# Differential attention in a hybrid layer: the sample's heads in a stream of their own, q and k split once, both maps' scores in one tile

## The chip, the core and the metric

The kernel runs on one core of a Trainium2 chip. The metric is the device time of that core in microseconds, the median of several executions. One further execution is taken by the hardware profiler; the page and every view of the trace quoted here come from that one.

## What is computed

One step of a hybrid layer: 512 prompt tokens and 32 tokens of a sample with 512 cached positions, side by side in a width of 544 (`TOK`). A combined projection feeds branch A (differential attention), branch B (RWKV-7 time mixing) and gates; both branches are projected, merged, projected again, and a gated convolutional FFN follows. All of it is fp32. The change is in branch A, 8 heads, and in one helper that branch B uses too. What branch A computes for each head:

```python
def diff_attend(q, k, v, lam, mask):
    s = jnp.einsum('bqhcd,bkhcd->bchqk', q, k) * (DA_HEAD_DIM ** -0.5)
    if mask is not None:
        s = jnp.where(mask, s, -1e30)
    p = jax.nn.softmax(s, axis=-1)
    pd = p[:, 0] - lam * p[:, 1]
    return jnp.einsum('bhqk,bkhd->bqhd', pd, v)
...
    o = rmsnorm(o, da_subln) * (1.0 - lam_init)
    o_da = o.reshape(B, T, DA_WIDTH) @ w_o_da
```

`c` runs over the two softmax maps; q and k have 64 rows per map, v has 128. The prompt's queries go in four blocks of 128; block i sees keys 0 to 128(i+1), in chunks of 64 (`mask`). The sample's 32 queries see 512 cached and 32 new keys, with no mask.

## The kernel before, in words

**Products.** TensorE multiplies fp32 as three matmuls of a rounded part and a remainder (`hi`, `lo`). A dense product (`dense_g`, line 202) loads a weight tile of 128x512 on the SP queue (`wr`, three buffers), casts it on ScalarE (`wh`), subtracts on VectorE or GpSimd (`wl`) and issues the matmuls into `psd`. Its rows read `psd<-…`.

**The planner.** `Flow` (line 93) runs generators, called streams. A stream yields the time at which it may go on, or a mark it waits for; when no stream is due, `Flow` takes one step of dense work. The time is a model's (`PE.now`). In the attention the dense work is first what is left of the gates' and the input's projections (`fillers`), then `orw_g` (branch B's output projection, its input loaded by `load_z`). A scheduler behind it reorders instructions on each engine by its own model; the built order is then fixed.

**Attention** (`attention`, line 1308) is one stream. For each head h: `tokens` transposes v; for each block i, `scores` (line 1284) issues, for each map m, two matmuls into a PSUM tile of its own (`sc0`, `sc1`, each one bank), a mask write, a maximum (line 1298), an exponential with a sum (line 1299); then the pair is combined to `pd`. While that runs, `weighted` transposes the block before (`pdt`) and multiplies by v into `po`; after block 3 `attend_norm` (line 1113) takes the root of the mean square by an integer guess and four Newton steps (`rsqrt_tiny`, line 260). `finish_head` transposes the normed head (`on`) and puts it as `dh`, `dl` (`put_z`) for the last projection, `w_oda`. The pool `ap` has one buffer for each name where none is given.

**Loading a head** (`load_head`, line 1253). q and k lie in DRAM as 128 rows a head, 64 for each map. For each map m the rows are loaded twice, to both halves of a tile: Q holds the rounded part in one half and the remainder in the other, so that one matmul against K's rounded part in both halves takes two of the three products:

```python
for f in (hi, lo):
    nc.sync.dma_start(out=raw[f, :], in_=d[h, hi, :])
x = ap.tile([128, TOK], F32R, name=f"x{n}{m}")
A.copy(out=x, in_=raw)
if t == 0:
    V.tensor_tensor(out=x[lo, :], in0=raw[lo, :], in1=x[lo, :].bitcast(F32), op=ALU.subtract)
```

That is eight loads of 64x544 and v, four casts and four differences a head, with a raw tile and a cast tile for each of q and k and each map (`rQ0`, `xQ0`, `rK0`, `xK0`, …). For K the raw tile becomes the remainder (`rK` in `sc<-rK,xQ`). `load_head(h + 1)` is called after head h's scores, and the planner adds 6.5 us before the next scores may come.

**The sample** (`attend_sample(g)`, line 1177) handles four heads at once, packed in quarters of the partitions. It is called inside the same stream after heads 3 and 7, after `weighted` and `finish_head` of that head; `load_caches` loads the keys (`kc`). It uses the same PSUM tiles `sc0`, `sc1` and `po`.

**The start.** `load_z` (line 1126) loads eight tiles `zr` (two buffers), casts each and subtracts on GpSimd.

Of the kernel before, what the change touches and what calls it, by code (L numbers as in the profile page):

```python
# [26 lines left out]
SEQ = 512  # L27
# [134 lines left out]
def tile_hybrid_layer(  # L162
# [97 lines left out]
    def rsqrt_tiny(pool, x, n, tag):  # L260

        p = x.shape[0]
        yt = pool.tile([128, 16], F32, name=tag + "y", bufs=2)
        tt = pool.tile([128, 16], F32, name=tag + "t", bufs=2)
        y, t = yt[:p, :n], tt[:p, :n]
        V.tensor_scalar(out=y.bitcast(I32), in0=x.bitcast(I32), scalar1=-0.5, scalar2=1597463007.0,
                        op0=ALU.mult, op1=ALU.add)
        for _ in range(4):
            V.tensor_tensor(out=t, in0=y, in1=y, op=ALU.mult)  # L269
            V.scalar_tensor_tensor(out=t, in0=t, scalar=-0.5, in1=x, op0=ALU.mult, op1=ALU.mult)  # L270
            V.scalar_tensor_tensor(out=y, in0=t, scalar=1.5, in1=y, op0=ALU.add, op1=ALU.mult)
        return y
# [839 lines left out]

    def attend_norm(po, rz0, n):

        ssq = ap.tile([128, 4], F32, name="ssq", bufs=2)
        on = ap.tile([128, 4, 128], F32, name="on")
        for i in range(n):
            A.activation(out=on[:, i, :], in_=po[:, i, :], func=AF.Square, scale=rz0[:, i:i + 1], accum_out=ssq[:, i:i + 1])
        V.tensor_scalar(out=ssq[:, :n], in0=ssq[:, :n], scalar1=128.0 * EPS, scalar2=None, op0=ALU.add)
        rr = rsqrt_tiny(ap, ssq[:, :n], n, "at")  # L1120
        V.tensor_tensor(out=rr, in0=rr, in1=rz0[:, :n], op=ALU.mult)
        V.tensor_tensor(out=on[:, :n], in0=po, in1=rr.unsqueeze(2).to_broadcast([128, n, 128]), op=ALU.mult)
        return on


    def load_z(pool, src, h, l, eng):
        for k in range(KT):
            zr = pool.tile([128, TOK], F32, name="zr", bufs=2)
            nc.sync.dma_start(out=zr, in_=src[k])
            A.copy(out=h[:, k, :], in_=zr)  # L1130
            eng.tensor_tensor(out=l[:, k, :], in0=zr, in1=h[:, k, :].bitcast(F32), op=ALU.subtract)
# [45 lines left out]
    def attend_sample(g):  # L1177
# [6 lines left out]
        yield PE.now + 1.0  # L1184
        sc = [pssc.tile([128, 512], F32, name=f"sc{m}") for m in range(2)]
        kc = caches[g]
        for e, hh in enumerate(hs):
            for m in range(2):
                PE.matmul(sc[m][32 * e:32 * e + 32, :], qks[m * 64:m * 64 + 64, 0, hh, :],
                          kc[m * 64:m * 64 + 64, e, :], start=True, stop=True,  # L1190
# [9 lines left out]
        nm = ap.tile([128, 2], F32, name="nm", bufs=3)  # L1200
        nm2 = ap.tile([128, 2], F32, name="nm2")
        for m in range(2):
            V.tensor_reduce(out=nm[:, m:m + 1], in_=sc[m], axis=AX.X, op=ALU.max, negate=True)
            V.tensor_reduce(out=nm2[:, m:m + 1], in_=scn[m][:, 0:32], axis=AX.X, op=ALU.max, negate=True)
# [4 lines left out]
        for m in range(2):  # L1209
            A.activation(out=E[:, m, 0:PAST], in_=sc[m], func=AF.Exp, bias=nm[:, m:m + 1], scale=1.0,  # L1210
                         accum_out=Z4[:, 0, m:m + 1])
# [22 lines left out]
        A.copy(out=pdtn, in_=ps[0:32, 0:128])  # L1234
        yield max(PE.now + 1.5, po_free[0])
        po = pssc.tile([128, 4, 128], F32, name="po")
        Q4 = [slice(32 * e, 32 * e + 32) for e in range(4)]
# [4 lines left out]
        for e, q in enumerate(Q4):  # L1242
            PE.matmul(po[q, 0, :], pdtn[:, q], vs[:, e, :], start=False, stop=True, tile_position=(0, 32 * e))
        on = attend_norm(po[:, 0:1, :], rz1[:, 0:1], 1)
        po_free[0] = PE.now + 4.0
        yield PE.now + 5.0
# [6 lines left out]
    def load_head(h):  # L1253

        vt = ap.tile([128, TOK], F32, name="vt")
        nc.sync.dma_start(out=vt, in_=v_d[h])
        Q, KH, KL = [], [], []
        for m in range(2):
            hi, lo = slice(m * 64, m * 64 + 64), slice(64 - m * 64, 128 - m * 64)
            for t, (d, n) in enumerate(((q_d, "Q"), (k_d, "K"))):  # L1260
                kept = ap.tile([128, TOK], F32R if t else F32, name=f"r{n}{m}")
                raw = kept.bitcast(F32) if t else kept
                for f in (hi, lo):
                    nc.sync.dma_start(out=raw[f, :], in_=d[h, hi, :])
                x = ap.tile([128, TOK], F32R, name=f"x{n}{m}")
                A.copy(out=x, in_=raw)
                if t == 0:
                    V.tensor_tensor(out=x[lo, :], in0=raw[lo, :], in1=x[lo, :].bitcast(F32), op=ALU.subtract)
                    Q.append(x)
                else:  # L1270
                    V.tensor_tensor(out=kept, in0=raw, in1=x.bitcast(F32), op=ALU.subtract)
                    KH.append(x)
                    KL.append(kept)
        return vt, Q, KH, KL

# [8 lines left out]
    def scores(i, Q, KH, KL, rz):  # L1284

        nk = 128 * (i + 1)
        sc = [pssc.tile([128, 512], F32, name=f"sc{m}") for m in range(2)]
        nm = ap.tile([128, 2], F32, name="nm", bufs=3)
        E = ap.tile([128, 2, 512], F32, name="E", bufs=2)
        Z = ap.tile([128, 4], F32, name="Z", bufs=3)  # L1290
        for m in range(2):
            qb = slice(i * 128, (i + 1) * 128)

            n = max(nk, 256)
            PE.matmul(sc[m][:, 0:n], Q[m][:, qb], KH[m][:, 0:n], start=True, stop=False)
            PE.matmul(sc[m][:, 0:n], Q[m][:, qb], KL[m][:, 0:n], start=False, stop=True)
            V.memset(sc[m][0:64, nk - 64:nk], -1e30)
            V.tensor_reduce(out=nm[:, m:m + 1], in_=sc[m][:, 0:nk], axis=AX.X, op=ALU.max, negate=True)
            A.activation(out=E[:, m, 0:nk], in_=sc[m][:, 0:nk], func=AF.Exp, bias=nm[:, m:m + 1], scale=1.0,
                         accum_out=Z[:, m:m + 1])  # L1300
# [8 lines left out]
    def attention():  # L1309
# [36 lines left out]
        nxt = load_head(0)  # L1346
        load_caches(0)
        yield PE.now + 9.0
        for h in range(HEADS):
            vt, Q, KH, KL = nxt  # L1350
            vtok = tokens(vt)
            rz = ap.tile([128, 4, 2], F32, name="rz", bufs=2)
            for i in range(4):
# [8 lines left out]
                prev = h, i, pd, ready, vtok, rz  # L1362
            if h + 1 < HEADS:
                nxt = load_head(h + 1)
                sc_free = max(sc_free, PE.now + 6.5)
            if h % 4 == 3:
                yield from weighted(*prev)
                prev = None
                yield from finish_head()
                yield from attend_sample(h // 4)  # L1370
                if h + 1 < HEADS:
                    load_caches(h // 4 + 1)

    flow.run([attention()], att_dense)
    att_dense.finish()
# [286 lines left out]
```

## Time and profile before

| | us |
|---|---|
| median of the three runs | 1378.87 |
| the runs | 1372.31, 1378.87, 1379.1 |
| the profiled execution | 1372.92 |
| its span in the trace | 1371.1 |
| mean granted TensorE clock | 0.942 |
| TensorE busy in the span | 1271.1 (93%) |
| VectorE, ScalarE, GpSimd busy | 884.9, 587.3, 229.6 |

The page's 40 slices are 34.3 us each. The attention is in slices 19 to 26, some 627 to 868 us. A digit is the busy share of an engine in tenths; PEclk the granted clock in tenths. The chain that ended last is 75% TensorE and 14% VectorE:

```profile
PE   7799999799989999998898977799999999999996
PEclk9999888799989899999899996799999999999999
```

### The profile page before, as it was taken

The numbers are of one execution on the slowest core, as the hardware profiler recorded it, in microseconds if no ns is written. First come the engines' busy times: TensorE is split into PE (matmuls) and PEld (weight loads), VectorE is DVE, ScalarE is ACT, GpSimd is POOL, SyncE is SP. The second block draws the span as 40 slices with busy tenths as digits, with TensorE's granted clock in tenths as the row PEclk, the third lists the DMA queues.
The fourth block names the chain that finished last, engine by engine and source line by source line (L and its number), as shares of the span: only waits on it lengthen the run. The fifth ranks groups of instructions, "written<-read, shape, count | busy, mean of one in ns | idle before, by whom it ended". The sixth has DMA issues, their size and how long they took to land.

```text
span 1371.1 us, 29786 instructions
## 1 busy us (share of the span) xinstructions
PE 1271.1 (93%) x12014; PEld 1206.1 (88%) x12014; DVE 884.9 (65%) x1835; ACT 587.3 (43%) x1184; POOL 229.6 (17%) x264
## 2 busy tenths in 40 slices
PE   7799999799989999998898977799999999999996
PEld 7798898798878899988798964799999999999996
DVE  6857559765779233862767675566878778873323
ACT  5655544464412333334664464234544444453220
POOL 6600102111213101224202100000111111111111
PEclk9999888799989899999899996799999999999999
DMA  5255555154685354537662530345222222234321
GB/s 173 77 162 161 166 172 164 59 152 131 204 257 172 93 144 125 165 102 219 181 200 91 158 95 32 97 157 165 95 86 86 93 85 90 88 112 140 102 79 65
DMA packets 135465, 178.01 MB, mean 130 GB/s; under 512 B 41248, under 2 KB 64416, under 8 KB 135328
## 3 DMA queue, kind: packets, MB, share of 16 engines
q1 hardware_dynamic: 122256, 154.86, 37.5%
q10 hardware_dynamic: 13072, 21.26, 4.7%
q8 instruction: 94, 1.54, 0.5%
q14 instruction: 43, 0.35, 0.1%
HBM read 138.39 MB, written 37.41 MB: 128 GB/s over the span
## 4 chain that ended last, share of the span: by engine, by line
PE 75%; DVE 14%; ACT 4%; issue 3%; DMA 2%; POOL 1%; SPq 0%; DVEq 0%; ACTq 0%; POOLq 0%
PE psd L88 59%; PE misc L88 5%; PE psq L88 3%; PE psy L88 2%; PE po L88 2%; PE sc L88 2%; PE tp L92 1%; PE misc L92 1%; DVE XT L680 1%; DVE itmp L489 1%; DMA q_d<-qt 1%; DVE NP L635 1%; DVE Xp L491 1%; DMA zr<-z_d 1%; DVE att L269 0%
## 5 line engine op out<-in xcount | busy, mean ns | idle before, releaser
L218 ACT CAST wh<-wr 128x512 fp32r<-128x512 f32 (+1 forms) x316 | 193.1, 617 | 368.1 <-PE psd L88 321.4
L88 PE MATMUL psd<-h_h,wh 128*128 128x272 f32 x976 | 300.5, 308 | 0.4
L88 PE MATMUL psd<-h_h,wl 128*128 128x272 f32 x976 | 292.7, 301 | 2.8 <-POOL wl L219 2.6
L88 PE MATMUL psd<-h_l,wh 128*128 128x272 f32 x976 | 293.3, 301 | 0.2 <-DVE h_l L443 0.2
L219 DVE TENSOR_TENSOR wl<-wr,wh 128x512 fp32r<-128x512 f32 x230 | 157.4, 688 | 114.1 <-ACT wh L218 109.1
L88 PE MATMUL psd<-xgh,wl 128*128 128x272 f32 x704 | 204.0, 290 | 0.0
L88 PE MATMUL psd<-xgh,wh 128*128 128x272 f32 x704 | 203.0, 288 | 0.0
L88 PE MATMUL psd<-xgl,wh 128*128 128x272 f32 x704 | 202.2, 287 | 0.0
L88 PEld LDWEIGHTS psd<-h_h,wh 128*128 128x128 f32 x976 | 193.7, 198 | 6.2 <-issue 2.3
L88 PEld LDWEIGHTS psd<-h_h,wl 128*128 128x128 f32 x976 | 193.0, 198 | 5.3 <-POOL wl L219 3.0
L88 PEld LDWEIGHTS psd<-h_l,wh 128*128 128x128 f32 x976 | 193.9, 199 | 2.8 <-issue 1.4
L219 POOL TENSOR_TENSOR wl<-wr,wh 128x512 fp32r<-128x512 f32 x86 | 120.6, 1406 | 400.3 <-ACT wh L218 327.7
L88 PEld LDWEIGHTS psd<-xgl,wh 128*128 128x128 f32 x704 | 132.7, 188 | 0.0
L88 PEld LDWEIGHTS psd<-xgh,wl 128*128 128x128 f32 x704 | 132.3, 188 | 0.0
L88 PEld LDWEIGHTS psd<-xgh,wh 128*128 128x128 f32 x704 | 132.2, 188 | 0.1
L88 PE MATMUL psd<-ah,wh 128*128 128x272 f32 x352 | 101.7, 289 | 0.0
L88 PE MATMUL psd<-ah,wl 128*128 128x272 f32 x352 | 101.5, 288 | 0.0
L88 PE MATMUL psd<-al,wh 128*128 128x272 f32 x352 | 101.4, 288 | 0.0
L88 PE MATMUL psd<-mh,wh 128*128 128x272 f32 x256 | 76.2, 298 | 0.0
L88 PE MATMUL psd<-mh,wl 128*128 128x272 f32 x256 | 74.7, 292 | 0.0
L88 PE MATMUL psd<-ml,wh 128*128 128x272 f32 x256 | 74.6, 291 | 0.0
L1460 POOL COPY cvo<-uf 128x2 f32<-128x2 f32 x88 | 36.8, 449 | 220.3 <-DVE uf L1457 220.3
(366 smaller groups left out, 2592.8 us busy)
## 6 DMA issues: line engine op xcount, KB each, us to landing
wr<-w_in SPq DMA_DIRECT2D x132, 256.0 KB, 3.1
wr<-w_up SPq DMA_DIRECT2D x88, 256.0 KB, 2.8
wr<-w_down SPq DMA_DIRECT2D x40, 256.0 KB, 2.7
bkL<-bk_d SPq DMA_DIRECT2D x16, 512.0 KB, 5.0
ar_d<-ar SPq DMA_DIRECT2D x8, 544.0 KB, 3.1
t_d<-qt ACTq DMA_DIRECT2D x16, 272.0 KB, 2.9
rQ<-q_d SPq DMA_DIRECT2D x32, 136.0 KB, 3.8
rK<-k_d SPq DMA_DIRECT2D x32, 136.0 KB, 2.9
```

The source lines that it names most:

```text
L88: ins = self.pe.matmul(out, lhsT, rhs, **kw)
L92: ins = self.pe.transpose(out, in_, ident)
L218: A.copy(out=wh[:, :n], in_=raw)
L219: le.tensor_tensor(out=wl[:, :n], in0=raw, in1=wh[:, :n].bitcast(F32), op=ALU.subtract)
L489: V.tensor_tensor(out=tv, in0=X[:, :, 0:i, 0:i], in1=N[:, :, i, 0:i].unsqueeze(2).to_broadcast([128, 2, i, i]), op=ALU.mult)
L491: V.tensor_reduce(out=X[:, :, 0:i, i], in_=tv, axis=AX.X, op=ALU.add)
L635: V.transpose(out=xz[r0:r0 + 32].rearrange("p m a -> p a m"), in_=Xp[r0:r0 + 32, 0:16, :])
L680: V.transpose(out=XT[r0:r0 + 32, :, 32 * b:32 * b + 32].rearrange("p m i -> p i m"), in_=Xp[r0:r0 + 32].rearrange("p a i -> p i a"))
L1460: G.tensor_copy(out=cvo[:, t, :, w], in_=u[:, 512 + w::32])
```

## The change

1. `rsqrt_tiny` takes three Newton steps instead of four. It is used in `attend_norm`, in branch B's group norm and for its sample.
2. `load_z`: `zr` has one buffer instead of two.
3. `load_head`: q and k are each loaded once as 128x512 (`raw`), cast (`hi`) and subtracted (`lo`) once, and twelve copies of 64x512 between on-chip tiles, on the SP queue, place the parts (four for `Q`, eight for `KH` and `KL`). All six tiles have one buffer. It is called for h+1 at the start of head h, and the 6.5 us are gone.
4. `scores`: both maps lie in one PSUM tile of two banks; one mask write and one maximum serve both, and the exponentials come after.
5. `samples()` is a second stream: sample 0 is due after head 1's scores, sample 1 after head 4's; it loads its own caches. Its product goes to the pool of transposes (`tp`) instead of `po`, and its normed tile has a name of its own (`son`).

```diff
-        for _ in range(4):
+        for _ in range(3):
...
-            zr = pool.tile([128, TOK], F32, name="zr", bufs=2)
+            zr = pool.tile([128, TOK], F32, name="zr")
...
-        sc = [pssc.tile([128, 512], F32, name=f"sc{m}") for m in range(2)]
+        sc = pssc.tile([128, 2, 512], F32, name="sc")
...
+        V.tensor_reduce(out=nm, in_=sc, axis=AX.X, op=ALU.max, negate=True)
         for m in range(2):
-            V.tensor_reduce(out=nm[:, m:m + 1], in_=sc[m], axis=AX.X, op=ALU.max, negate=True)
...
-        yield max(PE.now + 1.5, po_free[0])
-        po = pssc.tile([128, 4, 128], F32, name="po")
+        yield PE.now + 1.5
+        po = misc().rearrange("p (a v) -> p a v", a=4)
...
-        Q, KH, KL = [], [], []
...
+        x = {n: ap.tile([128, 2, SEQ], F32R, name=n) for n in ("Q", "KH", "KL")}
+        F = [slice(0, 64), slice(64, 128)]
+        for d, places in ((q_d, (("Q", 0), ("Q", 1))), (k_d, (("KH", None), ("KL", None)))):
+            raw = ap.tile([128, SEQ], F32, name="raw")
+            nc.sync.dma_start(out=raw, in_=d[h, :, 0:SEQ])
+            hi, lo = [ap.tile([128, SEQ], F32R, name=n) for n in ("hi", "lo")]
+            A.copy(out=hi, in_=raw)
+            V.tensor_tensor(out=lo, in0=raw, in1=hi.bitcast(F32), op=ALU.subtract)
+            for m in range(2):
+                for part, (n, flip) in zip((hi, lo), places):
+                    for f in range(2) if flip is None else ((m + flip) % 2,):
+                        nc.sync.dma_start(out=x[n].bitcast(F32)[F[f], m, :], in_=part.bitcast(F32)[F[m], :])
+        return vt, x["Q"], x["KH"], x["KL"]
...
         for m in range(2):
-            qb = slice(i * 128, (i + 1) * 128)
-
-            n = max(nk, 256)
-            PE.matmul(sc[m][:, 0:n], Q[m][:, qb], KH[m][:, 0:n], start=True, stop=False)
-            PE.matmul(sc[m][:, 0:n], Q[m][:, qb], KL[m][:, 0:n], start=False, stop=True)
-            V.memset(sc[m][0:64, nk - 64:nk], -1e30)
-            V.tensor_reduce(out=nm[:, m:m + 1], in_=sc[m][:, 0:nk], axis=AX.X, op=ALU.max, negate=True)
-            A.activation(out=E[:, m, 0:nk], in_=sc[m][:, 0:nk], func=AF.Exp, bias=nm[:, m:m + 1], scale=1.0,
+            PE.matmul(sc[:, m, 0:n], Q[:, m, qb], KH[:, m, 0:n], start=True, stop=False)
+            PE.matmul(sc[:, m, 0:n], Q[:, m, qb], KL[:, m, 0:n], start=False, stop=True)
+        V.memset(sc[0:64, :, nk - 64:nk], -1e30)
+        V.tensor_reduce(out=nm, in_=sc[:, :, 0:nk], axis=AX.X, op=ALU.max, negate=True)
+        for m in range(2):
+            A.activation(out=E[:, m, 0:nk], in_=sc[:, m, 0:nk], func=AF.Exp, bias=nm[:, m:m + 1], scale=1.0,
                          accum_out=Z[:, m:m + 1])
...
-            if h + 1 < HEADS:
-                nxt = load_head(h + 1)
-                sc_free = max(sc_free, PE.now + 6.5)
-            if h % 4 == 3:
-                yield from weighted(*prev)
-                prev = None
-                yield from finish_head()
-                yield from attend_sample(h // 4)
-                if h + 1 < HEADS:
-                    load_caches(h // 4 + 1)
-
-    flow.run([attention()], att_dense)
+            flow.mark(("head", h))
+        yield from weighted(*prev)
+        yield from finish_head()
+
+    def samples():
+        for g, h in ((0, 1), (1, 4)):
+            load_caches(g)
+            yield ("head", h), 0.0
+            yield from attend_sample(g)
+
+    flow.run([attention(), samples()], att_dense)
```

**Where the dense work ends, TensorE.** In the program before, the last dense rows before the tail stand ahead of head 5's last block (`sc…<-xK…,xQ… 128x512`); the weighted product of that head and head 6's first scores follow:

```order
L88 MATMUL psd<-dl,wh 128x272
L88 MATMUL psd<-dh,wl 128x272
L88 MATMUL sc_10064<-xK_9858,xQ_9852 128x512
L88 MATMUL sc_10064<-rK_9855,xQ_9852 128x512
L88 MATMUL po<-vtok,pdt 128x128
L92 MATMUL tp<-cst,on 128x128 x4
L92 MATMUL tp<-cst,pd 128x128 x2
L88 MATMUL sc_10125<-xK_10102,xQ_10096 128x256
```

With the change the dense rows end ahead of head 5's first block (`128x256`), and the second sample's scores (`sc<-kc,qks`) stand inside head 5 (the two maps' matmuls read alike):

```order
L88 MATMUL psd<-dl,wh 128x272
L88 MATMUL psd<-dh,wl 128x272
L88 MATMUL sc<-KH,Q 128x256
L88 MATMUL sc<-KL,Q 128x256
L88 MATMUL sc<-KH,Q 128x256
L88 MATMUL sc<-KL,Q 128x256
L88 MATMUL sc<-kc,qks 32x512 x8
L92 MATMUL tp<-cst,pd 128x128
```

The long run of dense rows now ends four blocks of scores earlier, and the second sample moved from after head 7 to head 5.

**The start, SP.** Before, the loads of head 1 (`rQ_8182` and on) and their weights stood in this order; a K load of head 1 waits until head 0's matmuls have read the tile:

```order
L1129 DMA zr<-z_d 128x544
L1264 DMA rK_7882<-k_d 64x544 x2
L1175 DMA kc<-kcache 128x4x512
L1256 DMA vt<-v_d 128x544
L1264 DMA rQ_8182<-q_d 64x544 x2
L1264 DMA rQ_8194<-q_d 64x544 x2
L1264 DMA rK_8188<-k_d 64x544 x2
L217 DMA wr<-w_in 128x512 x3
```

With the change, from the fifth `zr` on:

```order
L1129 DMA zr<-z_d 128x544
L1267 DMA KH<-hi 64x512 x2
L1267 DMA KL<-lo 64x512 x2
L1129 DMA zr<-z_d 128x544
L1260 DMA raw<-q_d 128x512
L217 DMA wr<-w_in 128x512 x3
L1129 DMA zr<-z_d 128x544
L1260 DMA raw<-k_d 128x512
L217 DMA wr<-w_in 128x512 x3
L1151 DMA mg<-t_d 128x544 x2
```

The weights moved ahead of head 1's copies, and the `zr` loads moved behind head 0's copies.

**A head's boundary, SP.** The copies for head 1 with the change, from map 1's Q on:

```order
L1267 DMA Q<-hi 64x512
L1267 DMA Q<-lo 64x512
L1255 DMA vt<-v_d 128x544
L217 DMA wr<-w_in 128x512
L1267 DMA KH<-hi 64x512 x2
L1267 DMA KL<-lo 64x512 x2
L1267 DMA KH<-hi 64x512 x2
L1267 DMA KL<-lo 64x512 x2
L1260 DMA raw<-q_d 128x512
L217 DMA wr<-w_orw 128x512 x3
```

All twelve copies of a head stand in the one queue that loads the weights, which had eight loads there before.

## Rows read from the trace of the kernel before

**Rows 1.** Windows: busy us by engine (instructions), clock, DMA share, GB/s.

```profile
535.00:625.00 90.00, 86.68 (x938) 81.67 (x937) 60.21 (x122) 29.70 (x59) 19.80 (x15) 1.00 0.39 127
645.00:668.00 23.00, 17.87 (x79) 14.58 (x77) 14.49 (x35) 12.66 (x34) 6.42 (x5) 0.64 0.67 206
668.00:801.50 133.50, 124.60 (x990) 118.69 (x988) 93.61 (x288) 73.08 (x211) 19.59 (x15) 0.97 0.50 150
801.50:832.50 31.00, 20.91 (x121) 16.24 (x120) 25.64 (x96) 21.80 (x68) 0.00 (x0) 0.89 0.25 73
832.50:868.30 35.80, 22.50 (x132) 14.04 (x132) 13.63 (x56) 9.34 (x31) 0.00 (x0) 0.55 0.15 46
```

**Rows 2.** Windows, dense products' tile psd alone.

```profile
668.00:801.50 133.50, 96.30 (x667) 89.00 (x667) 6.89 (x16) 4.33 (x11) 0.97 0.50 150
801.50:832.50 31.00, 3.16 (x12) 2.11 (x12) 0.00 (x0) 0.00 (x0) 0.89 0.25 73
832.50:868.30 35.80, 4.15 (x13) 2.76 (x13) 0.00 (x0) 0.00 (x0) 0.55 0.15 46
```

**Rows 3.** Timeline of TensorE, tail: start, duration, instructions [idle before].

```profile
801.12 0.40 PE L88 MATMUL sc<-rK,xQ 128*128 128x512 f32 x1
...
809.81 0.36 PE L88 MATMUL sc<-xK,xQ 128*128 128x256 f32 x1
...
812.12 0.44 PE L88 MATMUL sc<-xK,xQ 128*128 128x384 f32 x1 [1.33 <-ACT E L1299]
...
814.54 0.50 PE L88 MATMUL sc<-xK,xQ 128*128 128x512 f32 x1 [1.35 <-ACT E L1299]
...
843.66 2.78 PE L88 MATMUL po<-vtok,pdt 128*128 128x128 f32 x14
...
853.69 0.82 PE L88 MATMUL psd<-dh,wh 128*128 128x272 f32 x2
...
868.26 0.59 PE L88 MATMUL psd<-dh,wh 128*128 128x272 f32 x1 [0.46 <-ACT dh L1141]
```

**Rows 4.** DMA issues: KB each, median us from issue to landing.

```profile
rQ<-q_d SPq DMA_DIRECT2D x32, 136.0 KB, 3.8
...
zr<-z_d SPq DMA_DIRECT2D x8, 272.0 KB, 3.1
...
cs<-tw SPq DMA_DIRECT2D x2, 136.0 KB, 2.4
```

**Rows 5.** Timeline of SP, start of attention.

```profile
643.50 0.33 SPq L1129 DMA_DIRECT2D zr<-z_d  x1
...
658.11 1.53 SPq L217 DMA_DIRECT2D wr<-w_in  x3
```

**Rows 6.** Instructions around zr: ns min/median/max, first and last start.

```profile
L1130 ACT CAST mh<-zr x8: 637/646/648, 628.5 to 646.6; 128x544 fp32r<-128x544 f32 x8
L1131 POOL TENSOR_TENSOR ml<-zr,mh x8: 1341/1353/1362, 629.5 to 647.3; 128x544 fp32r<-128x544 f32 x8
```

**Rows 7.** Lines of VectorE, 801.5 to 832.5 us: busy, mean ns, idle before.

```profile
L1298 DVE TENSOR_REDUCE nm<-sc 128x1 f32<-128x512 f32 x4 | 2.7, 685 | 0.0
...
L1298 DVE TENSOR_REDUCE nm<-sc 128x1 f32<-128x256 f32 x4 | 1.5, 402 | 0.1
...
L1297 DVE MEMSET sc<- 64x64 f32 x16 | 1.8, 112 | 2.5 <-PE sc L88 2.4
```

**Rows 8.** Lines of ScalarE, the same stretch.

```profile
L1299 ACT ACTIVATE E<-sc,nm 128x512 f32<-128x512 f32 x5 | 3.5, 692 | 0.3 <-DVE att L269 0.3
L1299 ACT ACTIVATION_READ_ACCUMULATOR E<-sc,nm 128x1 f32 x16 | 3.3, 207 | 0.0
...
L1299 ACT ACTIVATE E<-sc,nm 128x128 f32<-128x128 f32 x4 | 1.5, 373 | 0.7 <-PE sc L88 0.7
```

**Rows 9.** Lines of VectorE, the same stretch: the root's products.

```profile
L269 DVE TENSOR_TENSOR att<-aty 128x4 f32<-128x4 f32 x7 | 1.1, 155 | 0.1
```

**Rows 10.** What SP's queue waits for, 630 to 870 us: total, times, longest.

```profile
SPq L1264 <- PE sc L88: 33.3, 9, 8.0
```

More of the change, by code (lines that the diff above doesn't have):

```diff
@@ L1111, in tile_hybrid_layer, with attend_norm @@
     fpool[0] = ap
-    def attend_norm(po, rz0, n):
+    def attend_norm(po, rz0, n, name="on"):
         ssq = ap.tile([128, 4], F32, name="ssq", bufs=2)
-        on = ap.tile([128, 4, 128], F32, name="on")
+        on = ap.tile([128, n, 128], F32, name=name)
         for i in range(n):
@@ L1188, in attend_sample @@
             for m in range(2):
-                PE.matmul(sc[m][32 * e:32 * e + 32, :], qks[m * 64:m * 64 + 64, 0, hh, :],
+                PE.matmul(sc[32 * e:32 * e + 32, m, :], qks[m * 64:m * 64 + 64, 0, hh, :],
                           kc[m * 64:m * 64 + 64, e, :], start=True, stop=True,
@@ L1209, in attend_sample @@
         for m in range(2):
-            A.activation(out=E[:, m, 0:PAST], in_=sc[m], func=AF.Exp, bias=nm[:, m:m + 1], scale=1.0,
+            A.activation(out=E[:, m, 0:PAST], in_=sc[:, m, :], func=AF.Exp, bias=nm[:, m:m + 1], scale=1.0,
                          accum_out=Z4[:, 0, m:m + 1])
@@ L1243, in attend_sample @@
             PE.matmul(po[q, 0, :], pdtn[:, q], vs[:, e, :], start=False, stop=True, tile_position=(0, 32 * e))
-        on = attend_norm(po[:, 0:1, :], rz1[:, 0:1], 1)
-        po_free[0] = PE.now + 4.0
+        on = attend_norm(po[:, 0:1, :], rz1[:, 0:1], 1, "son")
         yield PE.now + 5.0
@@ L1256, in load_head @@
         nc.sync.dma_start(out=vt, in_=v_d[h])
-        Q, KH, KL = [], [], []
[L1258 to L1274, printed above, removed]
+        x = {n: ap.tile([128, 2, SEQ], F32R, name=n) for n in ("Q", "KH", "KL")}
[11 more added lines that the diff above has]
+        return vt, x["Q"], x["KH"], x["KL"]
     def tokens(vt):
@@ L1286, in scores @@
         nk = 128 * (i + 1)
-        sc = [pssc.tile([128, 512], F32, name=f"sc{m}") for m in range(2)]
+        sc = pssc.tile([128, 2, 512], F32, name="sc")
         nm = ap.tile([128, 2], F32, name="nm", bufs=3)
@@ L1290, in scores @@
         Z = ap.tile([128, 4], F32, name="Z", bufs=3)
+        qb = slice(i * 128, (i + 1) * 128)
+        n = max(nk, 256)
         for m in range(2):
-            qb = slice(i * 128, (i + 1) * 128)
-            n = max(nk, 256)
-            PE.matmul(sc[m][:, 0:n], Q[m][:, qb], KH[m][:, 0:n], start=True, stop=False)
-            PE.matmul(sc[m][:, 0:n], Q[m][:, qb], KL[m][:, 0:n], start=False, stop=True)
-            V.memset(sc[m][0:64, nk - 64:nk], -1e30)
-            V.tensor_reduce(out=nm[:, m:m + 1], in_=sc[m][:, 0:nk], axis=AX.X, op=ALU.max, negate=True)
-            A.activation(out=E[:, m, 0:nk], in_=sc[m][:, 0:nk], func=AF.Exp, bias=nm[:, m:m + 1], scale=1.0,
+            PE.matmul(sc[:, m, 0:n], Q[:, m, qb], KH[:, m, 0:n], start=True, stop=False)
[4 more added lines that the diff above has]
+            A.activation(out=E[:, m, 0:nk], in_=sc[:, m, 0:nk], func=AF.Exp, bias=nm[:, m:m + 1], scale=1.0,
                          accum_out=Z[:, m:m + 1])
@@ L1346, in attention @@
         nxt = load_head(0)
-        load_caches(0)
         yield PE.now + 9.0
@@ L1350, in attention @@
             vt, Q, KH, KL = nxt
+            if h + 1 < HEADS:
+                nxt = load_head(h + 1)
             vtok = tokens(vt)
```

## The prediction, made before the changed kernel ran

> **What bounds the kernel now.** I read the windows by stage first, then each engine in the stretch where TensorE is not full. TensorE is the bound wherever a dense product stands by: from 668.0 to 801.5 us, where six heads' and one sample's attention runs between dense products, it is busy 124.6 of 133.5 us [rows 1]. Two stretches are not full. At the start, 645 to 668, it is busy 17.9 of 23.0 us at a granted clock of 0.64. At the end there is no dense work left: 31.0 us for heads 6 and 7 and 35.8 us for head 7's rest and the second sample, with 12 and 13 dense matmuls in them [rows 1, 2]. That tail, 66.8 us, is a chain: scores, maximum, exponentials, weighted product. TensorE's timeline shows it waiting for E on ScalarE before most blocks [rows 3]. So the change is decided by three questions: how long the tail's chain gets, how much stands in it, and what becomes of the start.
>
> **The change part by part.** The order of TensorE's instructions, shown with the change, says where the cover ends. Total dense work is the same, but now it ends with head 5's first scores instead of its last: heads 5, 6 and 7 stand uncovered, with the second sample's scores inside head 5, and 27 dense matmuls in the tail where 25 were. Heads 6 and 7 took 15.5 us each before (31.0 / 2).
>
> *Copies at a head's boundary.* Before, each map has raw and cast tiles of its own, and the next head's raw rows are loaded early; from head 5's last score matmul to head 6's second block are 8.3 us (801.5 to 809.8) [rows 3]. Now one buffer each holds raw, hi, lo, Q, KH and KL. Q's copies wait for the last score matmul of the head before; k's cast into hi waits until Q's two copies from hi have landed; KH's and KL's copies wait for the cast and the difference. Nothing of that can run ahead. A copy between on-chip tiles exists once in the trace: 136 KB, 2.4 us to land; the 136 KB q loads take 3.8 [rows 4]. I take 2.4, the same kind and size, and keep 3.8 as the upper bound; 2.0 is my lower one, an estimate, a little under the row. An issue on SP costs 0.51 (three in 1.53) [rows 5]; I take 0.54, bounds 0.33 (the zr issue) and 0.54. From the last score matmul: the third Q copy is issued at 1.1, lands at 3.5; the cast (0.65 for 544 columns, so 0.62 for 512) [rows 6] ends at 4.2; eight more issues, the last at 8.0, landed at 10.4; the last first-block matmul ends at 10.7.
>
> *One tile for both maps.* The mask and one maximum over both maps: a maximum takes 0.40 for 256 columns and 0.685 for 512 [rows 7], a slope of 0.14 per 128, so 256, 512, 768 and 1024 columns cost 0.40, 0.69, 0.97 and 1.25; bounds are that and twice the single one (1.37 for the last). The mask is 0.11 for one map; I take 0.2. Each exponential has an accumulator read of 0.21 behind it, 0.37 + 0.21 at 128 columns and 0.69 + 0.21 at 512 [rows 8]. The next block's matmuls wait for both exponentials. Block 0: 0.6 + 2 x 0.58 + 0.4 for hand-overs, so at 12.8. Block 1: matmuls 0.9, then 0.9, 1.4 and 0.4, some 3.5. Block 2: 1.2, 1.1, 1.6, 0.4, so 4.3. Block 3's matmuls 1.4. The put of the head before stands ahead of block 1's exponentials on ScalarE, 0.7. The sum is 12.8 + 3.5 + 4.3 + 1.4 + 0.7 = 22.7; with the norm of the head before ahead of the first mask on VectorE, **23 us per uncovered head** against 15.5.
>
> Before, head 6's third block starts 2.3 us after its second and the fourth 2.4 us after that, because each map's bank comes free with its own exponential [rows 3]. The page "PSUM — Partial Sum Buffer" of the Trainium skill (section "Summary: rules for kernel authors") would have semaphores guard PSUM by bank and the matmul write into another bank than the one being read; one tile over two banks goes against it. With the maps released apart, as in the rows, blocks 1 and 2 would cost 4.7 instead of 7.8, 3 us less a head, and the sum below would be 9 lower, +5.
>
> *The samples.* The second sample leaves the end. It adds in head 5's chain: matmuls 1.5, maximum 1.6, exponentials 2.8 on the engines on which head 5 waits, and about 2.5 for its square, norm and copies behind: 8 us (between 3, if all but the exponentials lies in gaps, and 14.6, the 853.7 to 868.3 that it held after head 7's norm [rows 3]).
>
> *After the last head.* Block 3's mask, maximum and exponentials 3.5; normalisation 1.3; transposes, copies and products 2.8: 7.6 to the last product (13.9 before, 832.5 to 846.4, with ten and six sample matmuls between [rows 1, 3]); then the norm to the first dense product, 7.3 before (846.4 to 853.7), less 0.5 for the root, and 0.2 put on for a hand-over: 7.0. In all 14.6.
>
> *Roots in three steps.* Three VectorE instructions fewer, 0.155 each [rows 9]: 0.5 at each norm. Only the last one is on the end's chain, and it is in the 7.0. In the recurrence, whose norms also have them, TensorE is busy 86.7 of 90 us [rows 1] and dense work hides it: nothing; if that cover went, at most 0.5 for each of four norms.
>
> *Tail.* 3 x 23, less 7 of cover (35 dense matmuls stand between head 4's last scores and head 5's first, 96.3 / 667 = 0.144 each [rows 2], so 5.0, and 2 for transposes and products), plus 8, plus 14.6: 85 us against 66.8, **+18**. Head 5's own matmuls leave the covered stretch: the part of it that is not dense is 124.6 − 96.3 = 28.3 us for six heads and a sample, **−4**.
>
> *Start.* Some 79 matmuls at 0.144 need 11 of the 23 us, so 12 are lost there. The stall goes with weights that stood on SP behind head 1's K loads (first weight issue 658.1) [rows 5]. Now the weights stand ahead and two more weight tiles come before the first scores, good for up to −8. Against it, zr has one buffer: load 3.1, cast 0.65, difference 1.35 on GpSimd [rows 4, 6], 5.1 us for each of the eight tiles in a row, with head 0's loads and copies between on SP. The eighth, issued at 643.5 before [rows 5], comes at about 660 instead, and the o_rw products need all eight; weights queued behind it move with it. I take **0**, between −8 and +6.
>
> The changed casts (two instead of four a head) and loads lie beside dense work: nothing there; without cover they are in the 23. The sum is +18 − 4 + 0 = **+14**. The profiled execution took 1372.92, so 1386.9. The runs shown lie at 1372.3 and about 1379, the median 1378.87 being 5.95 above the profiled one; I add half of that: **1390**.
>
> **The rivals.** *A, faster:* the boundary is not a serial chain. If copies are issued while earlier ones land and casts overlap with them, so that a boundary stays near the 8.3 of before, its second block starts 4.5 us earlier than at 12.8, a head takes 18.5 and the tail 71, so +4 − 4 there; if the start then gives its 8, **1368**, counted as the forecast is. It decides once the boundary (last score to next head's second block) is under 9 us. For it: dense products end just as late if stalls go. Against: the single buffers, each a wait in the order of the queues.
>
> *B, no change:* the boundary is as forecast, but the start's stall goes and nothing replaces it: +14 − 9 = +5, **1381**. For it: weights stand ahead of copies now. Against: the zr chain.
>
> *C, slower still:* waiting copies on SP hold up weights behind them in the covered stretch. SP already waits 33.3 us there for score matmuls ahead of its rQ and rK loads [rows 10]. With 3 us at each of four boundaries, **1402**. Against: the order puts most weights ahead of the copies.
>
> That the change does only half of what it says is in the forecast: the second sample is not between covered heads, the order has it in the tail.
>
> **How the numbers follow.** Forecast 0.50, A 0.20, B 0.18, C 0.12. The forecast's own range: issues at 0.33 take 1.9 a head away, −6; landings of 3.8 add 2.8 a head, +8; so 1384 to 1398. A measurement of this kernel tells some 0.5%, 6.9 us, from no change. Faster is A, 0.20; same is B and a twentieth of the forecast, 0.20; slower the rest, 0.60. The range leaves A out: from B's lower side, 1372, to C's upper, 1406.
>
> **What would show it.** Right: after the dense rows end, three heads of about 23 us, with TensorE idle some 10 us at each boundary until a KL copy lands; ScalarE's k cast waiting for a Q copy; the second sample inside head 5; the tail at about 85 us. Wrong: a boundary under 9 us, dense products that reach beyond head 5, a start whose stall stays or grows past 6 us, or the gain or loss coming from the stretches outside 625 to 890 us.

## The result and the profile after

The changed kernel takes 1386.42 us (median of 6, 1385.77 to 1391.37) against 1374.45 for the kernel before, timed beside it on the same chip: ratio 1.009, 95% interval 1.0062 to 1.0117. It is slower by 12 us. Below, *cover* is dense work that TensorE can do while a head's chain waits, a head without it is *bare*, and the *tail* is the stretch from the last dense product ahead of the bare heads to the next steady dense work. The profiled executions stand 14.8 us apart, 1387.72 (span 1385.9) and 1372.92 (span 1371.1). Four stretches, cut at events that both programs have, say where:

| stretch of the profiled execution | before | after | difference |
|---|---|---|---|
| to the first of branch B's last sample products (`misc<-sg,arL`) | 618.0 | 624.8 | +6.7 |
| from there to the last dense product ahead of the tail | 183.5 | 176.2 | −7.3 |
| the tail, to the first steady dense product | 66.8 | 82.2 | +15.4 |
| the rest | 502.8 | 502.8 | 0 |

The windows view of the changed kernel (columns as in [rows 1]), with the tail in one row:

```profile
645.00:668.00 23.00, 15.63 (x98) 14.71 (x96) 1.81 (x3) 5.82 (x11) 7.86 (x6) 0.85 0.68 201
668.00:800.93 132.93, 127.02 (x1000) 118.38 (x1000) 85.75 (x220) 74.07 (x215) 22.79 (x17) 0.97 0.66 195
800.93:883.08 82.15, 46.47 (x252) 34.43 (x252) 43.46 (x141) 32.26 (x109) 0.00 (x0) 0.74 0.32 84
```

and the dense products alone in that tail:

```profile
800.93:883.08 82.15, 6.98 (x28) 5.00 (x28) 0.00 (x0) 0.00 (x0) 0.74 0.32 84
```

Against [rows 1, 2] the tail is 82.15 us instead of 66.8, with 28 recorded dense matmuls instead of 25: it is longer and as bare. The start window is no better (15.6 us busy instead of 17.9, at a granted clock of 0.85 instead of 0.64); set later by the 6.7 us of the first stretch, 651.8 to 674.8, it has 13.9. TensorE's timeline through the tail (as [rows 3]):

```profile
791.59 0.40 PE L88 MATMUL sc<-KL,Q 128*128 128x512 f32 x1
...
800.64 0.29 PE L88 MATMUL psd<-dh,wl 128*128 128x272 f32 x1
...
806.36 1.96 PE L88 MATMUL sc<-kc,qks 64*32 64x512 f32 x16 [2.25 <-DVE lo L1263]
...
822.15 0.39 PE L88 MATMUL sc<-KL,Q 128*128 128x512 f32 x1
...
844.62 0.39 PE L88 MATMUL sc<-KL,Q 128*128 128x512 f32 x1
...
855.99 0.58 PE L88 MATMUL sc<-KL,Q 128*128 128x256 f32 x1 [0.58 <-DMA KL<-lo]
859.16 0.58 PE L88 MATMUL sc<-KH,Q 128*128 128x256 f32 x1 [2.59 <-ACT E L1294]
...
867.88 0.39 PE L88 MATMUL sc<-KL,Q 128*128 128x512 f32 x1
...
883.08 1.05 PE L88 MATMUL psd<-dh,wh 128*128 128x272 f32 x3 [0.78 <-ACT dh L1141]
```

These rows are the last score matmul of head 4, the last dense product, the second sample, the ends of heads 5 and 6, head 7's last first-block matmul and its second block, its end, and the first dense product behind the tail. Head 5 with the sample takes 30.5 us (792.0 to 822.5), head 6 22.5, head 7 23.3; 8.9 us of head 5 lie under cover; from head 7's end to dense work are 14.8. Together 82.2.

One boundary, from head 6's end at 845.0, in SP's timeline:

```profile
845.04 0.47 SPq L1267 DMA_DIRECT2D Q<-hi  x1
...
846.83 0.59 SPq L1267 DMA_DIRECT2D Q<-lo  x1
849.24 1.10 SPq L1267 DMA_DIRECT2D KH<-hi  x2
...
852.96 1.24 SPq L1267 DMA_DIRECT2D KL<-lo  x2
```

and in ScalarE's, k's cast and what ended its wait:

```profile
848.59 0.62 ACT L1262 CAST hi<-raw 128x512 fp32r<-128x512 f32 x1 [0.52 <-DMA Q<-hi]
```

SP issues Q's four copies one after the other, then nothing until k's cast (848.59, released by a Q copy's landing) is through; then eight issues at 0.62 each, the last ending at 854.2. The landing, by the DMA view, is as that of the one copy of before [rows 4]:

```profile
KH<-hi SPq DMA_DIRECT2D x32, 128.0 KB, 2.5
...
Q<-hi SPq DMA_DIRECT2D x16, 128.0 KB, 2.3
```

KL's last copy releases TensorE at 856.0, 11.0 us after head 6's last scores. VectorE's timeline shows that it is not free for head 7's mask then; the previous head's norm ends ahead of it:

```profile
856.85 0.69 DVE L1122 TENSOR_TENSOR on<-po,aty 128x512 f32<-128x512 f32 x1
857.56 0.17 DVE L1291 MEMSET sc<- 64x128 f32 x1
857.75 0.42 DVE L1292 TENSOR_REDUCE nm<-sc 128x2 f32<-128x256 f32 x1
```

so that head 7's second block starts at 859.2, 14.2 us into the head ([rows 3] have 8.3). The norm ends 1 us behind the first block's last matmul. The merged maximum in the tail, VectorE's lines:

```profile
L1292 DVE TENSOR_REDUCE nm<-sc 128x2 f32<-128x1024 f32 x3 | 3.7, 1225 | 0.1
...
L1292 DVE TENSOR_REDUCE nm<-sc 128x2 f32<-128x768 f32 x3 | 2.9, 958 | 0.1
...
L1292 DVE TENSOR_REDUCE nm<-sc 128x2 f32<-128x256 f32 x3 | 1.3, 424 | 0.1
```

At the start, TensorE's timeline shows two waits, for weights and for exponentials:

```profile
656.08 0.60 PE L88 MATMUL psd<-h_h,wh 128*128 128x272 f32 x1 [5.42 <-ACT wh L218]
...
670.29 0.58 PE L88 MATMUL sc<-KH,Q 128*128 128x256 f32 x1 [3.82 <-ACT E L1294]
```

and the `zr` loads (ns, then first and last start) reach to 670.4 instead of 643.5 [rows 5]; counted from branch B's event in the first row of the table, 45.6 us instead of 25.5:

```profile
L1129 SPq DMA_DIRECT2D zr<-z_d x8: 320/326/382, 631.0 to 670.4; - x8
```

### The profile page after: what moved, and what is told of

It is laid out like the page before. It is cut to its first block, busy times and chain, and to the rows that moved or that the text cites. A ratio compares the mean times of both kernels' runs of the same rounds, so it can differ in the third digit from the quotient of the medians.

```text
span 1385.9 us, 29732 instructions
## 1 busy us (share of the span) xinstructions
PE 1273.7 (92%) x12014; PEld 1209.4 (87%) x12014; DVE 866.9 (63%) x1708; ACT 577.0 (42%) x1168; POOL 229.7 (17%) x264
## 4 chain that ended last, share of the span: by engine, by line
PE 76%; DVE 12%; ACT 4%; DMA 4%; issue 3%; SPq 1%; POOL 1%; DVEq 0%; ACTq 0%; POOLq 0%
PE psd L88 60%; PE misc L88 5%; PE psq L88 3%; PE psy L88 2%; PE sc L88 2%; PE misc L92 2%; PE po L88 1%; PE tp L92 1%; DVE NP L675 1%; ACT E L1294 1%; DVE XT L680 1%; DMA arL<-ar_d 1%; DMA t_d<-qt 1%; DMA bk_d<-bk 0%; DVE cs L526 0%
```

## The experiments

Twelve kernels ran. Ratios are to the kernel before, timed beside each; stage times are from each kernel's own profile, one for each kernel. The kernel before had medians of 1370 to 1374 us beside them, so that kernels are compared with each other by their ratios.

**e1, four root steps** in the changed kernel's `rsqrt_tiny`:

```diff
-        for _ in range(3):
+        for _ in range(4):
```

> The changed kernel with four Newton steps again. In the changed kernel's trace the last product of branch B's sample (misc<-sg,arL) stands at 624.8 us against 618.0 before, with the same number of TensorE instructions ahead of it. Theory 1: the shorter roots move the order on VectorE, and this costs about 6.7 us; then the stage ends near 618 again and the kernel takes 1380, the tail's 82 us unchanged. Theory 2: the stage differs from execution to execution; then it stays within 3 us of 624.8 or anywhere between, and the kernel takes 1386 within 3.

Measured: 1389.04 us, ratio 1.0146 (1.0103 to 1.0189); the stage ends at 618.9. The stage came back, and the kernel did not get faster: in its trace the tail is 85.2 us, 3 longer, and the stretch ahead of the tail is 3 longer too. The bare heads 6 and 7 take 23.9 and 24.8 us instead of 22.5 and 23.3. At head 7's boundary, which begins at 844.0 here, KL's copy releases TensorE as soon as in the changed kernel (11.0 us),

```profile
854.95 0.58 PE L88 MATMUL sc<-KL,Q 128*128 128x256 f32 x1 [0.58 <-DMA KL<-lo]
```

but VectorE comes to head 7's mask only 13.6 us into the head, instead of 12.6, since the norm with its fourth step stands ahead:

```profile
857.58 0.17 DVE L1291 MEMSET sc<- 64x128 f32 x1
```

Of that 1 us the step's three instructions are 0.6; the norm also starts 0.4 later. So the shorter root helps at a bare boundary too, not at the end alone. What the change's row of 624.8 is worth is seen from the kernels with three steps: the eleven others that were profiled have this event at 618.7 to 622.7, with the same order of instructions on TensorE and VectorE up to it (but for two pairs of neighbouring products in e8). Three kernels' rows (before, changed, e2; first and last start at the end):

```profile
L88 PE MATMUL misc<-sg,arL x16: 205/276/276, 618.0 to 619.6; 128*128 128x32 f32 x16
```

```profile
L88 PE MATMUL misc<-sg,arL x16: 205/276/276, 624.8 to 626.4; 128*128 128x32 f32 x16
```

```profile
L88 PE MATMUL misc<-sg,arL x16: 205/276/276, 618.9 to 620.5; 128*128 128x32 f32 x16
```

The 6.7 us are thus for the most part not the shorter roots'; a cost of up to 5 us there is not excluded, and a gain of them in the whole is not shown, for the intervals of e1 and the changed kernel overlap. Whether the rest belongs to this one execution or to this program stays open: the changed kernel has one trace, and that execution lies only 1.3 us above the median of six.

**e2, the old load_head** in the changed kernel, called at the start of the head before:

```diff
-        x = {n: ap.tile([128, 2, SEQ], F32R, name=n) for n in ("Q", "KH", "KL")}
...
+        Q, KH, KL = [], [], []
+        for m in range(2):
...
+                for f in (hi, lo):
+                    nc.sync.dma_start(out=raw[f, :], in_=d[h, hi, :])
```

> The changed kernel with the old load_head (eight loads, four casts, no copies; called at the start of the head before). Theory: the copies at the boundary cost some 7 us a head and let the dense products run out early; in this kernel's order dense products stand between all heads' scores, 60 behind head 7's last. Then the tail of 82 us shrinks to the end's chain, some 15 to 25 us, and the kernel takes 1335 to 1355. Rival: TensorE's work is what counts and the copies lie beside it; then the kernel stays within 1380 to 1390.

Measured: 1340.09 us, ratio 0.9784 (0.9743 to 0.9825). Giving up the new load_head alone turns 12 us of loss into 30 to 33 of gain. (It takes back the copies and the single buffers together; only e10 and e12 below part them, and only for some of the tiles.) The tail is gone: in the windows view, over the time where the changed kernel's tail begins, TensorE is 93% busy at full clock.

```profile
800.93:835.00 34.07, 31.65 (x240) 29.94 (x239) 22.96 (x66) 17.23 (x52) 1.29 (x1) 1.00 0.23 75
```

**e3, a score tile for each map**, copies as changed:

```diff
-        sc = pssc.tile([128, 2, 512], F32, name="sc")
+        sc = [pssc.tile([128, 512], F32, name=f"sc{m}") for m in range(2)]
```

> The changed kernel with a score tile for each map again, maximum and exponentials per map; copies as changed. Theory: each uncovered head loses 3 us by the merged tile, and its longer chain lets dense work run out earlier. The order has dense products up to head 6's third block and the second sample between covered heads. Then the tail is one head of 20, and 15 behind it, some 40 us instead of 82, about 10 us more of work in the covered part: 1350 to 1362. Rival: the merged tile saves as much on VectorE as it costs, 1380 to 1390.

Measured: 1371.3 us, ratio 1.0003 (0.9976 to 1.0029): between the two. The cover reaches head 6 as the order says and the tail is 47.9 us (819.0 to 866.9), but TensorE's timeline shows the uncovered head no shorter:

```profile
829.97 0.40 PE L88 MATMUL sc<-KL,Q 128*128 128x512 f32 x1
...
842.85 0.58 PE L88 MATMUL sc<-KH,Q 128*128 128x256 f32 x1 [2.09 <-ACT E L1293]
...
853.35 0.45 PE L88 MATMUL sc<-KL,Q 128*128 128x512 f32 x1
```

From head 6's last scores (830.4) to head 7's (853.8) are 23.4 us, with the merged tile 23.3. The 3 us a head are not there; in this kernel, too, the norm of the head before stands ahead of the first mask. What e3 saves on the changed kernel, 12 us by the ratios and 15 by the medians, it saves by a later end of the dense work: 200 us after branch B's event instead of 176, with a tail 34 us shorter.

**e4, the samples in the attention's stream**, after heads 3 and 7:

```diff
+            if h % 4 == 3:
+                yield from weighted(*prev)
+                prev = None
+                yield from finish_head()
+                yield from attend_sample(h // 4)
```

> The changed kernel with the samples called in the attention's stream again, after heads 3 and 7. Theory: the second sample costs 8 us inside head 5 and 15 to 17 at the end; the order ends the dense work after head 5 instead of ahead of it. The tail is two heads of 23, 15 for the last, and 15 to 17 for the sample: 76 to 78 against 82, with head 5's work of 4 back under cover: 1383 to 1387, so no change. Rival: the sample's place is what costs, 1372 or less.

Measured: 1397.24 us, ratio 1.0192 (1.0156 to 1.0228), 11 us above the changed kernel by the medians and 14 by the ratios: missed. The tail is 89.3 us (801.6 to 890.9). Its end is a little shorter than forecast, 27 us from head 7's last scores at 863.7 (7 to head 7's last product, 20 for its norm and the sample). TensorE's timeline at the first steady dense product behind the sample:

```profile
890.87 0.60 PE L88 MATMUL psd<-dh,wh 128*128 128x272 f32 x1 [0.46 <-ACT dh L1141]
```

What I had wrong is the cover: 16 dense products stand inside head 5, which is 2 us, not the head; 15 us of head 5 (to 816.3) are bare. So the stream is a part of the change that pays, 10 us or more here.

**e5, the planner's order pinned** on TensorE for the attention, copies as changed:

```diff
+    PE.pinned = True
     flow.run([attention(), samples()], att_dense)
```

> The changed kernel with TensorE's instructions of the attention kept in the planner's order, copies as changed; dense products then stand between all heads' scores (some 15 ahead of a head's first scores, 45 to 85 in each head, 234 behind the last), as with the old load_head in e2. Theory 1, the copies' own time: each boundary still takes 11 to 14 us of which 15 dense products hide 2, a head is bound by its chain of 23 us wherever it stands, heads 0 to 7 take some 190 us, and the kernel takes 1360 to 1372. Theory 2, only the order: where the dense work stands is what cost the time, and a chain between dense products costs nothing; then as e2, 1335 to 1345.

Measured: 1435.49 us, ratio 1.0467 (1.0411 to 1.0522). Theory 2 falls; theory 1 was far too mild: from head 0's first scores to head 7's last are 249 us, not 190. With few dense products at a boundary, TensorE waits there in every head (waits of TensorE over the attention: us, times, longest):

```profile
PE sc L88 <- DMA KH<-hi: 58.6, 15, 19.7
PE sc L88 <- DMA KL<-lo: 14.6, 16, 5.7
```

and in its timeline at one boundary:

```profile
772.42 0.39 PE L88 MATMUL sc<-KL,Q 128*128 128x512 f32 x1
...
781.23 0.55 PE L88 MATMUL sc<-KH,Q 128*128 128x256 f32 x1 [5.10 <-DMA KH<-hi]
...
784.90 0.55 PE L88 MATMUL sc<-KL,Q 128*128 128x256 f32 x1 [0.83 <-DMA KL<-lo]
```

From one head's last scores to the next one's last first-block matmul are 12.6 us, with transposes and products between. A head takes 30 to 37 us, not 23; that the fixed dense products behind the boundary lengthen its chain is the likely reason, but no run parts it.

**e6, zr in mg's slices** (eight buffers that cost no room):

```diff
-            zr = pool.tile([128, TOK], F32, name="zr")
+            zr = ring[:, k, :]
```

> The changed kernel with load_z's eight tiles loaded into the eight slices of mg, which is free then, instead of one buffer zr; nothing on SP waits for a difference on GpSimd there. Theory: the single buffer holds up two weight tiles and head 0's loads on SP; TensorE stalls 5.4 and 5.7 us at the start and runs at half clock behind them. Without it 5 to 8 us come back: 1378 to 1381. Rival: head 0's copies make the start's stall; then 1383 to 1389.

Measured: 1376.01 us, ratio 1.0041 (1.0024 to 1.0057), so 0.5% or 7 us below the changed kernel by the ratios (its median lies below the range expected, as the kernel before lies 4 us lower beside it). As expected in size, but only half by the mechanism. The eight loads are issued in one go; the stall for weights is still there, and the second one is gone. SP's timeline:

```profile
627.16 4.17 SPq L1129 DMA_DIRECT2D mg<-z_d  x8
```

and TensorE's:

```profile
654.17 0.60 PE L88 MATMUL psd<-h_h,wh 128*128 128x272 f32 x1 [6.43 <-ACT wh L218]
```

From branch B's last sample product to the last dense product it takes 173.4 us instead of 176.2, 3 less. The other 3 are in the tail, 79.4 instead of 82.2: 28 dense products stand between head 5's first scores and the sample in its order.

**e7 and e8** are e2 with e6's edit (`zr` in mg) and e2 with e3's edit (a score tile for each map).

> e2 (old load_head, else as changed) with load_z's tiles in the slices of mg. In e2 TensorE has one long stall without dense products at the start, 12.8 us from 647.5, and the weight loads behind a zr load are issued at 655.2. Theory: the single zr buffer makes it; 6 to 10 us come back, 1330 to 1334. Rival: the stall is head 0's own chain with nothing dense ready for another reason; then 1337 to 1343.

> e2 with a score tile for each map again: of the change there remain the samples' stream, the earlier call of load_head without 6.5 us, three root steps, and one zr buffer. Theory: under dense cover the merged tile's longer chain costs little; in e2 TensorE waits 7.1 us for the exponentials ahead of scores, so 0 to 5 us less, 1335 to 1341. Rival: VectorE is loaded with twice as many masks and maxima and holds up the dense sums: 1343 or more.

Measured: 1332.44 us (0.9718, 0.9686 to 0.975) and 1337.14 (0.9754, 0.9722 to 0.9787). Both lie in the range expected, though their intervals overlap that of e2; e8 gives no sign that the merged tile helps or hurts under cover. Nor does e7 show where the `zr` buffer costs its time: the 5 us wait of e2's trace at the start is gone, but head 0's last scores end 42 us after branch B's event in both, and the 7 us that e7's trace saves by head 7's end lie in the heads behind.

**e9, e2 with both edits**: the fastest kernel of the study.

> e7 (old load_head, zr tiles in mg's slices) with a score tile for each map: of the change there remain the samples' stream, the earlier call of load_head and three root steps. If the gains of e7 and e8 over e2 (8 and 3 us) stand side by side: 1326 to 1332. If they hide the same start stall: 1331 to 1336.

Measured: 1327.74 us, ratio 0.9701 (0.966 to 0.9742), 3% or 41 to 43 us below the kernel before. TensorE is 93% busy at full clock from 670 to 800 us and there is no tail; what is left is the start, as the windows show:

```profile
645.00:670.00 25.00, 20.72 (x120) 18.05 (x118) 14.34 (x43) 14.25 (x40) 3.85 (x3) 0.80 0.72 223
670.00:800.00 130.00, 121.38 (x986) 108.94 (x985) 112.38 (x374) 94.06 (x288) 20.03 (x14) 1.00 0.51 159
```

**e10 and e12, shorter waits at the boundary**, on e6. e10 gives Q two buffers, e12 gives hi and raw two; the remainder is written over raw.

```diff
-        x = {n: ap.tile([128, 2, SEQ], F32R, name=n) for n in ("Q", "KH", "KL")}
+        x = {n: ap.tile([128, 2, SEQ], F32R, name=n, bufs=2 if n == "Q" else 1) for n in ("Q", "KH", "KL")}
```

```diff
-            raw = ap.tile([128, SEQ], F32, name="raw")
+            lo = ap.tile([128, SEQ], F32R, name="lo", bufs=2)
+            raw = lo.bitcast(F32)
...
+            hi = ap.tile([128, SEQ], F32R, name="hi", bufs=2)
```

> e6 with two buffers for Q (the remainder lo is written over raw to make room), copies and merged tile as changed. Theory: the serial chain at the boundary is the cost; with Q's copies and k's cast done ahead it is eight issues and a landing, 7 us instead of 10.7 to 11.5. Heads 6 and 7 then take some 19.5 uncovered instead of 23, and the order has dense work to head 5's end, so that the tail is about 54 us instead of 80, with 5 to 10 more in the covered part: 1352 to 1364. Rival: the number of copies on SP counts, not their waits (twelve a head as before): 1372 to 1380.

> e6 with two buffers each for hi and for raw, over which lo is written; Q, KH and KL single. Casts and differences of the next head are done ahead, and the twelve copies wait together for the last score matmul: twelve issues and a landing, about 9.6 us, a head of 21 to 22 instead of 23. The order ends the dense work after head 5. Theory as for e10: two heads uncovered, 43, and 15: a tail of 58 us instead of 80: 1354 to 1366. Rival: as there, 1372 to 1380.

Measured: e10 1374.33 us, 1.0015 (0.9983 to 1.0047), a miss; e12 1365.74 us, 0.9978 (0.9951 to 1.0006), inside its range at the upper end, but not for the reason given: its bare heads take 22.1 and 23.3 us, not 21 to 22. TensorE's timeline in e10, head 6's end to head 7's:

```profile
834.64 0.40 PE L88 MATMUL sc<-KL,Q 128*128 128x512 f32 x1
...
842.87 0.41 PE L88 MATMUL sc<-KL,Q 128*128 128x256 f32 x1
847.21 0.58 PE L88 MATMUL sc<-KH,Q 128*128 128x256 f32 x1 [3.93 <-ACT E L1295]
```

and VectorE's in between:

```profile
844.44 0.17 DVE L1119 TENSOR_SCALAR ssq<-ssq 128x4 f32<-128x4 f32 x1 [5.10 <-ACT on L1118]
...
845.61 0.17 DVE L1292 MEMSET sc<- 64x128 f32 x1
...
847.13 0.69 DVE L1122 TENSOR_TENSOR on<-po,aty 128x512 f32<-128x512 f32 x1
```

The copies are 3 us sooner: the last first-block matmul ends at 843.3, 8.2 us after head 6's scores. But the norm of the head before starts at 844.4, holds VectorE until 847.8 with the mask in its midst, and the second block starts at 847.2, 12.2 after: the head takes 21.6 us, 1.7 less than in the changed kernel. In e12 TensorE's timeline shows the same:

```profile
823.73 0.40 PE L88 MATMUL sc<-KL,Q 128*128 128x512 f32 x1
...
833.27 0.58 PE L88 MATMUL sc<-KL,Q 128*128 128x256 f32 x1 [0.63 <-DMA KL<-lo]
838.27 0.58 PE L88 MATMUL sc<-KH,Q 128*128 128x256 f32 x1 [4.42 <-ACT E L1295]
```

Last first-block matmul done at 833.9, 9.7 us after head 6's scores; second block at 838.3, 14.1 after; the head 23.3 us, nothing less. The tails are shorter, since the dense work reaches further (54.4 us in e12 and 67.2 in e10, against 79.4 in e6), but the stretch ahead of the tail is longer by 15 and 10 us. Counted by heads, 6 of the 10 us that e12's trace saves on e6's lie ahead of all scores: its first scores come 31 us after branch B's last sample product, in e6 37. In e10 they come 41 us after it, behind 21 more dense rows than in e6.

**e11, e8 with the samples in the attention's stream** (e4's edit):

> e8 with the samples in the attention's stream again: the kernel before with load_head called a head earlier and without the planner's 6.5 us, three root steps and one zr buffer. Theory: what makes e2 and e8 faster than the kernel before is the earlier call, which lets heads follow each other faster and keeps dense work for the end; the order has dense products through head 7, and only the second sample stands uncovered behind it, about 15 us: 1346 to 1358. Rival: the samples' stream does it; then 1366 or more.

Measured: 1352.41 us, ratio 0.9878 (0.9837 to 0.9918). As expected: this is nearly the kernel before, with `load_head` called a head earlier and without the planner's 6.5 us, and it is 17 to 19 us faster. It has the three root steps and the single `zr` buffer too, so the 17 to 19 us are those of all these together. The samples' stream brings 15 to 17 more (e8).

## Why the prediction was right, and where its steps were not

The sum was +14; the profiled pair shows +14.8, the medians +12. The forecast of 1390 and its side hold. Point by point:

- **The cover's end, read from the order of instructions**: right. The dense products end with head 5's first scores, the sample stands inside head 5, and the tail is bare. It is the one reading on which all else hangs; e4 shows how it goes wrong when 16 rows are taken for a head's cover.
- **The copies at a boundary**: right step by step, up to the first block. Cast done 4.2 forecast, 4.2 measured (849.2); last issue 8.0 forecast, 8.6 measured, since an issue costs 0.62 and not 0.54; landing 2.4 forecast, 2.3 to 2.5; last first-block matmul 10.7 forecast, 11.6 measured at its end.
- **The merged maximum**: 0.40, 0.97 and 1.25 forecast, 0.42, 0.96 and 1.22 measured.
- **23 us a head**: 22.5 and 23.3, in part by two misses that cancel. The second block, forecast 12.8 us into the head, came at 13.7 and 14.2 (for head 7 the norm ended behind the copies); what follows took 9 us and not 10. **The sample in head 5**: 8 forecast, 7.5 measured (30.5 less 23). **After the last head**: 14.6 and 14.8. **Cover**: 7 and 8.9. **The tail**: 85 and 82.2.
- **"−4" for head 5's matmuls and "0" for the start**: together −7.3 measured, in the bounds that were given. The zr chain was as forecast in kind, and longer: the eighth load 45.6 us after branch B's event, not 42 (660 less the 618.0 of before). Of its own signs of being wrong one is there in part: the start's stall did not go (5.4 us for weights, 3.8 for exponentials), though none passes 6 us.
- **"In the recurrence … nothing"** for the roots: the profiled execution shows +6.7 there, which e1 and the other kernels show to be for the most part not the roots'. At the others' values the profiled pair would stand 9 to 13 us apart; the medians stand 12 apart. So two misses, −3 each in the tail and at the start, were covered by a stage that was costed at nothing: that the sum came out at +14 to the microsecond is luck.
- **"Only the last one is on the end's chain"**: wrong. The norm, and with it the root, stands on the chain at a bare boundary too: with the fourth step (e1) heads 6 and 7 are 1.4 and 1.5 us longer, in one trace each.
- **"3 us less a head" with the maps apart**: wrong. The step took head 6's second to fourth block in [rows 3] as the price of two banks. In e3 an uncovered head with the maps apart takes 23.4 us. What the maps apart gave in e3, 12 to 15 us, came by a later end of the dense work, and with the old `load_head` (e8 against e2) no difference is clear of the noise. The rule of the Trainium skill on banks ("PSUM — Partial Sum Buffer", "Summary: rules for kernel authors"), which guards PSUM by bank, gives no price for breaking it, and no run here shows one per head.
- **Rival A** (copies run ahead) fell: boundaries are 13.7 and 14.2 us, not under 9. **Rival B** (only the start's stall goes): the start did get some 3 us better, the tail as forecast, so it is a part, not the case. **Rival C** (weights held up by copies) is not seen in the covered stretch: TensorE is 127.0 of 132.9 us busy.

What the prediction did not see is why the cover ends sooner. It took the boundary's price where it was bare, three heads. e2 shows the larger one. In the changed kernel's built order 37 to 49 dense products stand between two heads' scores and 74 to 106 inside a head; in e2, which differs in `load_head` alone, 22 to 31 and 52 to 77. So some 130 a head are used up instead of 85, and none are left for heads 5 to 7. Taken back, the new `load_head` gives not the 12 us by which the change is slower, but 42 to 46 (e2 against the changed kernel). The kernel before pays in the same coin elsewhere: its order has 64 to 66 dense products between the heads under cover where e11, with the earlier call, has 15 to 23, and both have 189 between heads 3 and 4, where the first sample stands in the stream; e8, with the sample in a stream of its own, has 31 there.

## What to carry to other kernels

A serial wait under cover is not free: it uses up cover, and the price falls due where the cover ends. So count the filler work (here, the dense products) that stands at each such wait and see what is left for the end. Before splitting work "once" and placing it by copies, lay the chain from the last reader of the single buffer to the first user of the new one out in time; here two landings and twelve issues (11 us) took the place of loads that ran ahead. And when a wait is shortened, look at what else ends near it: here a norm that had ended 1 us behind the copies took about half of the gain back in e10 and all of it in e12.

## What the runs showed that was not expected

- Half of the change was good. The samples' own stream is worth 11 to 14 us (e4) or 15 to 17 (e11 against e8), and the earlier call of `load_head` with the planner's 6.5 us gone, together with three root steps and one `zr` buffer, 17 to 19 (e11); the new `load_head` hid both.
- Keeping the planner's order on TensorE (e5) cost 49 us by the medians and 52 by the ratios against the scheduler's for the same work.
- Branch B up to its last sample product, in the same order of instructions, took 618.7 to 624.8 us in twelve profiled kernels: a stage in which they do not differ moves by half the change's effect.
